# Eighteen up pairs in seven block products instead of fourteen, with one low part made by ScalarE and an accumulating DMA

## The chip, the core and the metric

The kernel runs on one core of a Trainium2 chip. Its engines are TensorE (PE in the rows), VectorE (DVE), ScalarE (ACT), GpSimd (POOL) and SyncE (SP); the last two here mostly issue DMAs. The metric is the device time of one execution in microseconds (us), lower is better. Three runs of the kernel before took 881.33, 883.00 and 883.19 us.

## The reference, cut to what matters

One layer of a streaming encoder over 512 tokens of width 1024, all in float32. The change lies in its last part, the feed-forward block:

```python
h = rmsnorm(x, ffn_pre_norm[l])
up = causal_dwconv(h @ w_ffn_up[l], ffn_conv_w[l], ffn_conv_b[l])   # 1024 -> 2 * 3072
f_gate, f_val = jnp.split(up, 2, axis=-1)
f = (jax.nn.gelu(f_gate, approximate=True) * f_val) @ w_ffn_down[l]
x = x + rmsnorm(f, ffn_post_norm[l])
```

## The kernel before, in words

Every float32 product is made of three products in a faster 32-bit format (float32r): an operand x is split into a high part (x rounded) and a low part (x minus the high part), and high x high, high x low and low x high are summed in PSUM. ScalarE makes the high part with a copy that rounds, VectorE the low part with a subtraction. Activations are kept split; weights come from HBM and are split on the way (`split`, `low` at L951).

The 6144 columns of the up projection are worked off in 24 pairs of 128 gate columns and 128 value columns. The weights of a pair are four blocks of 128 x 512: a11 and a12 (gate, first and second half of the 1024 inputs), a21 and a22 (value). The pairs 0 and 1 run ahead of the stretch looked at here. Each pair from 2 on is done in one of two ways:

- in eight block products (`eight`, L1049): each of the two outputs takes 24 matmuls of 512 columns, 48 in all, in four slots; a11 with a12, and a21 with a22, are split as one 1024-wide block;
- in seven block products (`seven`, L1014), a Winograd scheme on the 2 x 2 blocks of weights and activations: the sums s1, s2, s3, s4 of weight blocks stand beside a11, a12 and a22, the sums of activations are made once (`comb`), and each of the seven products is 12 matmuls of 256 columns, 84 in all. Six of them run in the pair's six slots in the order a11, s2, s4, s3, a12, s1; the seventh, with a22 (`last_product`, L998, the matmuls named ps<-L,a), runs within the next pair, and goes into a PSUM half that VectorE has read before (L1046).

`seven_of` (L908) says which pairs are done in seven: pair n = 4 + i unless i % 3 = 2, so 14 pairs; 2, 3, 6, 9, 12, 15, 18 and 21 are done in eight. A loop over the pairs (L1111) runs the slots; in each it splits the block that is used five slots later (`w_split`, L954; the split parts lie in a ring of six). For a seven, `w_split` also adds s2 = s1 + a11 on VectorE (L965, at a11), s4 = s2 + a12 (L968, at s2), and at s3 splits a22 as well, on ScalarE and VectorE. In slot 0 of pair n the weights of pair n + 2 are loaded (`pair_load`, L922, 1 MB, on SyncE's queue, L926) into the tile H that held those of pair n, so the load waits until all that was in it has been read. `pair_sums` (L931) makes s1 and s3 of pair n + 2 by DMA: a load from HBM on SyncE's queue (L940) and a second one that adds to it on GpSimd's (L942).

The outputs of a pair are finished while the next one runs: `gate_part` (a depthwise conv, ScalarE one tap, VectorE two, L226), `gelu_part`, `last_product`, `value_part` (L1002: one add, L1005, for a seven, the conv, and the product of gate and value, L866). For a seven VectorE also puts the partial products together with 256-wide adds (L1031, L1044, L1045, L1046). After pair 23 the down projection follows; `down_turn` finishes that pair in it.

TensorE and here ScalarE run in program order. VectorE, SyncE and GpSimd run in an order that a planner sets when the program is built: an instruction is put where the planner expects its inputs, ahead of ones that come earlier in the program if these are expected later. On the chip each engine's queue is then strictly in order. Waits between engines and for the reuse of buffers are set by the framework.

Of the kernel before, what the change touches and what calls it, by code (L numbers as in the profile page):

```python
# [8 lines left out]
F32 = mybir.dt.float32  # L9
# [3 lines left out]
ALU = mybir.AluOpType  # L13
# [9 lines left out]
NF = FF // P  # L23
# [33 lines left out]
def block_kernel(ctx: ExitStack, tc, x, slabs, wgate, pc, rows, out):  # L57
    nc = tc.nc
    V, A, PE = (InOrder(tc, e) for e in (nc.vector, nc.scalar, nc.tensor))
    G = nc.gpsimd  # L60
# [9 lines left out]
    def ps():  # L70
        return psum.tile([P, S], F32, tag="ps", name="ps")
# [16 lines left out]
    def mm3(acc, lhi, llo, rhi, rlo, start, stop):  # L88
        mm(acc, lhi, rhi, start, False)
        mm(acc, lhi, rlo, False, False)  # L90
        mm(acc, llo, rhi, False, stop)
# [770 lines left out]
    def f_gate(gt):  # L862
        A.activation(gt, gt, AF.Gelu_apprx_tanh)
# [34 lines left out]
    def block_product(out, w, b, start=False):  # L898

        for k in range(HK):  # L900
            c = slice(k * P, (k + 1) * P)
            for e, (u, v) in enumerate(((0, 0), (0, 1), (1, 0))):
                PE.matmul(out, lhsT=w[u][:, c], rhs=b[v][:, k, :], start=start and k == e == 0,
                          stop=k == HK - 1 and e == 2, skip_group_check=not start)

    seven_of = [False] * 4 + [i % 3 != 2 for i in range(NF - 4)] + [False]  # L908
    ORDER = "a11", "s2", "s4", "s3", "a12", "s1"
    blocks = [(n, q) for n in range(PLAIN, NF + 1)  # L910
              for q in (ORDER if seven_of[n] else ("a11", "a12", "a21", "a22"))]
# [32 lines left out]
    def place(kind, i):  # L944

        key = kind, i // 2
        if key not in room:
            room[key] = wts.tile([P, D], F32 if kind == "raw" else F32R, tag=kind, name=kind)
        return room[key][:, i % 2 * S:(i % 2 + 1) * S]

    def low(lo, src, hi):  # L951
        V.tensor_sub(lo, src, hi.bitcast(F32))  # L952

    def w_split(g):  # L954

        if g >= len(blocks):
            return
        n, q = blocks[g]
        b, i = blk[n], g % RING
        both = [place(kind, i) for kind in ("whi", "wlo")]  # L960
        b["w" + q] = both
        if seven_of[n]:
            if q == "a11":
                b["s2"] = place("raw", 4)
                V.tensor_add(b["s2"], b["s1"], b["a11"])  # L965
            elif q == "s2":
                b["s4"] = place("raw", 5)
                V.tensor_add(b["s4"], b["s2"], b["a12"])  # L968
            A.copy(both[0], b[q])
            low(both[1], b[q], both[0])  # L970
            if q == "s3":
                if not spare:
                    spare.append(work.tile([P, 2, 2, S], F32R, tag="M", name="a22", bufs=1))
                b["wa22"] = [spare[0][:, n % 2, e, :] for e in range(2)]
                A.copy(b["wa22"][0], b["a22"])
                low(b["wa22"][1], b["a22"], b["wa22"][0])
        elif q in ("a12", "a22"):
            hi, lo = (room[kind, i // 2] for kind in ("whi", "wlo"))
            src = b["raw"][:, 0:D] if q == "a12" else b["raw"][:, D:2 * D]
            A.copy(hi, src)  # L980
            low(lo, src, hi)
            if n == NF:
                splits[DOWN_SLAB + (q == "a22")] = hi, lo
# [7 lines left out]
    def gate_part(n):  # L991
        p = pr[n]
        p["g"] = conv(p["oa"], pcs[:, C_FCW + 3 * n:C_FCW + 3 * n + 3], C_FCB + n, 3)

    def gelu_part(n):
        f_gate(pr[n]["g"])

    def last_product(n):  # L998
        if seven_of[n]:
            block_product(pr[n]["z"][:, T1], blk[n]["wa22"], comb[3])  # L1000

    def value_part(n):  # L1002
        p = pr.pop(n)
        if seven_of[n]:
            V.tensor_add(p["ob"][:, T0], p["u2"], p["z"][:, T1])  # L1005
            w = negw[:, 3 * n:3 * n + 3]
        else:
            w = pcs[:, C_FCW + 3 * (NF + n):C_FCW + 3 * (NF + n) + 3]
        vt = conv(p["ob"], w, C_FCB + NF + n, 3)
        f_done(n, p["g"], vt)  # L1010
# [38 lines left out]
    def eight(n, old):  # L1049
        p = pr.setdefault(n, {})  # L1050
        for e, o in enumerate(("oa", "ob")):
            p[o] = acc = ps()
            for h in range(2):
                w = blk[n]["wa%d%d" % (e + 1, h + 1)]
                for k in range(HK):
                    c = slice(k * P, (k + 1) * P)
                    mm3(acc, w[0][:, c], w[1][:, c], h2T[0][:, HK * h + k, :],
                        h2T[1][:, HK * h + k, :], h == k == 0, h == 1 and k == HK - 1)
                if old:
                    if e == h == 0:  # L1060
                        gate_part(old)
                    elif e == 0:
                        gelu_part(old)
                        last_product(old)
                    elif h == 0:
                        value_part(old)
                yield

# [19 lines left out]
    for i in range(PLAIN):  # L1088
        acc = up_product()
        if i == 0:  # L1090
            pair_load(PLAIN)
            pair_load(PLAIN + 1)
        gt = conv(acc, pcs[:, C_FCW + 3 * i:C_FCW + 3 * i + 3], C_FCB + i, 3)
        if i == 0:
            w_split(0)
            w_split(1)
            for m in range(4):
                h_sum(m)
        else:
            for g in range(2, RING - 1):  # L1100
                w_split(g)
            h_split(1)
            h_split(2)
        acc = up_product()
        vt = conv(acc, pcs[:, C_FCW + 3 * (NF + i):C_FCW + 3 * (NF + i) + 3], C_FCB + NF + i, 3)
        f_gate(gt)
        f_done(i, gt, vt)
# [3 lines left out]
    for n in range(PLAIN, NF):  # L1111
        for slot, _ in enumerate((seven if seven_of[n] else eight)(n, old)):
            w_split(g + RING - 1)
            g += 1
            if slot == 0:
                pair_load(n + 2)
                pair_sums(n + 2)
            if n == PLAIN and slot in (1, 2):
                h_split(3 * (slot - 1))
            if n < NF - 1:  # L1120
                continue
            if slot == 2:
                stream.update(load=DOWN_SLAB + 2, split=DOWN_SLAB + 2, use=DOWN_SLAB)
                end[0] = slabs.shape[0]
                load_slab()
            elif slot == 3:
                f_split(0)
                f_split(1)
            elif slot == 5:
                f_split(2)  # L1130
                f_split(3)
        old = n
# [100 lines left out]
```

## Time and profile before

| | |
|---|---|
| median of three runs | 883.0 us |
| the profiled execution, its own time | 882.06 us |
| its span, first to last instruction | 880.4 us |
| TensorE busy | 864.7 us (98%) |
| VectorE busy | 587.4 us (67%) |
| ScalarE busy | 433.6 us (49%) |
| GpSimd busy | 28.4 us (3%) |
| granted TensorE clock, mean share of full speed | 0.996 |
| share of the chain that ended last: TensorE, VectorE, DMA, ScalarE | 75%, 11%, 7%, 5% |

A busy share is an average over stages with different limits, and matmuls are pipelined with modelled ends, so a busy TensorE is not one at its peak. The chain of work is followed back from the last instruction, at each step to what released it. Outside the stretch of pairs 4 to 23 the change touches nothing but the hand-over to the down projection.

### The profile page before, as it was taken

The page shows a single profiled execution, that of the slowest core. Times are in us where ns is not written, and L with a number is a line of the kernel's source. Part 1 is how long each engine was busy: PE and PEld are TensorE (multiplying, and loading weights), DVE is VectorE, ACT ScalarE, POOL GpSimd, SP SyncE. Part 2 cuts the span into 40 slices and gives each one's busy share as a digit, 9 for nine tenths or more (in the row PEclk, how much of TensorE's full clock was granted, in tenths as well). Part 3 has the DMA queues.
Part 4 walks back from the last instruction along what each step waited for, and adds up shares of the span by engine and source line. Part 5 has one row for each costly group of instructions (what it writes and reads, how often), then busy time and mean ns, then how long its engine had stood idle before and what let it go on. Part 6 is the DMA issues. An engine that isn't in the chain of part 4 may idle for free.

```text
span 880.4 us, 11591 instructions
## 1 busy us (share of the span) xinstructions
PE 864.7 (98%) x4554; PEld 739.7 (84%) x4554; DVE 587.4 (67%) x909; ACT 433.6 (49%) x714; POOL 28.4 (3%) x44
## 2 busy tenths in 40 slices
PE   7999999999999999999999999999999999999996
PEld 6888887888878888888888989889999899888885
DVE  6777657987875553444466797878978898743225
ACT  6444545578574443322365565445545556633222
POOL 0000000000000000000000101011011000000000
PEclk9999999999999999999999999999999999999999
DMA  6242223222334422222251837466556543422212
GB/s 225 96 146 96 96 94 110 90 84 79 119 103 174 154 96 96 87 99 101 97 191 25 212 127 195 126 180 170 165 144 181 156 127 113 144 96 95 96 48 96
DMA packets 36007, 108.47 MB, mean 123 GB/s; under 512 B 3632, under 2 KB 6896, under 8 KB 35440
## 3 DMA queue, kind: packets, MB, share of 16 engines
q1 hardware_dynamic: 30864, 99.34, 32.7%
q0 software_dynamic: 5088, 8.39, 5.7%
q8 instruction: 35, 0.57, 0.2%
q14 instruction: 20, 0.16, 0.1%
HBM read 103.49 MB, written 2.13 MB: 120 GB/s over the span
## 4 chain that ended last, share of the span: by engine, by line
PE 75%; DVE 11%; DMA 7%; ACT 5%; issue 2%; SPq 0%; DVEq 0%; ACTq 0%
PE ps L53 75%; DMA H<-slabs 5%; DVE wlo L952 2%; DVE tmp L226 2%; ACT whi L53 1%; DVE wlo L183 1%; ACT L L53 1%; DVE L L644 1%; DMA raw<-slabs 1%; ACT tmp L53 1%; DVE tmp L662 1%; DVE raw L965 0%; DMA wg<-wgate 0%; DVE L L638 0%; ACT junk L247 0%
## 5 line engine op out<-in xcount | busy, mean ns | idle before, releaser
L53 PE MATMUL ps<-H,whi 128*128 128x512 f32 x720 | 224.8, 395 | 0.4 <-DVE H L53 0.4
L183 DVE TENSOR_TENSOR wlo<-raw,whi 128x1024 fp32r<-128x1024 f32 x93 | 113.6, 1223 | 117.3 <-ACT whi L53 115.0
L53 ACT CAST whi<-raw 128x1024 fp32r<-128x1024 f32 (+1 forms) x144 | 127.5, 891 | 100.2 <-PE ps L53 96.6
L53 PE MATMUL ps<-C,whi 128*128 128x256 f32 (+1 forms) x656 | 166.5, 335 | 0.1
L53 PEld LDWEIGHTS ps<-H,whi 128*128 128x128 f32 x720 | 134.3, 188 | 30.3 <-issue 2.4
L53 PE MATMUL ps<-H,wlo 128*128 128x512 f32 x352 | 137.5, 391 | 0.4 <-DVE wlo L183 0.4
L53 PEld LDWEIGHTS ps<-C,whi 128*128 128x128 f32 x656 | 112.0, 190 | 12.6 <-DVE quad L1031 0.3
L53 PE MATMUL ps<-C,wlo 128*128 128x512 f32 (+1 forms) x360 | 122.2, 339 | 0.0
L53 PE MATMUL ps<-L,whi 128*128 128x256 f32 (+1 forms) x400 | 87.2, 300 | 0.0
L53 PE MATMUL ps<-whi,H 128*128 128x512 f32 x256 | 81.5, 394 | 0.0
L226 DVE SCALAR_TENSOR_TENSOR tmp<-ps,pcs,tmp 128x511 f32<-128x511 f32 (+2 forms) x100 | 74.5, 745 | 8.1 <-ACT tmp L53 7.2
L53 PEld LDWEIGHTS ps<-H,wlo 128*128 128x128 f32 x352 | 66.2, 188 | 15.3 <-DVE wlo L183 1.2
L53 PEld LDWEIGHTS ps<-C,wlo 128*128 128x128 f32 x360 | 68.3, 190 | 7.6
L53 PEld LDWEIGHTS ps<-L,whi 128*128 128x128 f32 x400 | 64.4, 191 | 2.5
L53 PEld LDWEIGHTS ps<-whi,H 128*128 128x128 f32 x256 | 48.1, 188 | 10.4 <-issue 0.5
L53 ACT ACTIVATE tmp<-tmp 128x512 f32<-128x512 f32 x36 | 22.7, 632 | 55.3 <-DVE tmp L226 55.3
L53 PE MATMUL ps<-wlo,H 128*128 128x512 f32 x128 | 49.8, 389 | 0.0
L952 DVE TENSOR_TENSOR wlo<-H,whi 128x512 fp32r<-128x512 f32 (+1 forms) x46 | 41.1, 894 | 9.7 <-ACT whi L53 9.6
L53 PE MATMUL ps<-L,wlo 128*128 128x256 f32 x168 | 47.5, 283 | 0.0
L53 ACT ACTIVATE tmp<-ps,halfb 128x512 f32<-128x512 f32 x32 | 21.5, 687 | 49.6 <-PE ps L53 49.6
L53 ACT ACTIVATE tmp<-ps,pcs 128x512 f32<-128x512 f32 x40 | 31.0, 776 | 27.9 <-PE ps L53 27.9
L53 PE MATMUL ps<-Y,whi 128*128 128x512 f32 x128 | 40.5, 397 | 0.2 <-DVE Y L200 0.2
(207 smaller groups left out, 1315.3 us busy)
## 6 DMA issues: line engine op xcount, KB each, us to landing
raw<-slabs SPq DMA_DIRECT2D x103, 512.0 KB, 3.2
H<-slabs SPq DMA_DIRECT2D x23, 1024.0 KB, 5.4
raw<-slabs SPq DMA_DIRECT2D x23, 256.0 KB, 3.8
raw<-slabs POOLq DMA_DIRECT2D x23, 256.0 KB, 6.5
quad<-x SPq DMA_DIRECT2D x8, 512.0 KB, 4.2
M<-acsD SPq DMA_DIRECT2D x4, 1024.0 KB, 4.6
out<-tmp SPq DMA_DIRECT2D x8, 256.0 KB, 2.0
third<-slabs SPq DMA_DIRECT2D x5, 256.0 KB, 6.3
```

What stands on the lines that cost most here:

```text
L53: return lambda *args, **kw: self.tc.keep_in_program_order(op(*args, **kw))
L183: V.tensor_sub(*late.pop(0))
L226: V.scalar_tensor_tensor(out=t[:, d:], in0=acc[:, :S - d], scalar=w[:, taps - 1 - d:taps - d], in1=t[:, d:], op0=ALU.mult, op1=ALU.add)
L644: V.tensor_tensor_scan(out=qq[:, e, :], data0=aa[:, e, :], data1=uu[:, e, :], initial=0.0, op0=ALU.mult, op1=ALU.add)
L662: V.tensor_mul(gl, gl, hs[i // 4][:, i % 4, :])
L952: V.tensor_sub(lo, src, hi.bitcast(F32))
```

## The change

`seven_of` is changed so that of the pairs 4 to 23 only 10 and 17 are done in eight products: 18 pairs in seven instead of 14, in three runs of six. In every seven the low part of a22 is no longer VectorE's subtraction: ScalarE writes minus the high part into the place of the low part, and a DMA issued by GpSimd adds a22 to it, from on-chip memory to on-chip memory. In a pair done in eight products the `last_product` of the pair before comes one slot later, after the third of four, and with it `value_part`, after the fourth.

```diff
-    seven_of = [False] * 4 + [i % 3 != 2 for i in range(NF - 4)] + [False]
+    seven_of = [False] * 4 + [i not in (6, 13) for i in range(NF - 4)] + [False]
...
                 b["wa22"] = [spare[0][:, n % 2, e, :] for e in range(2)]
-                A.copy(b["wa22"][0], b["a22"])
-                low(b["wa22"][1], b["a22"], b["wa22"][0])
+
+                hi, lo = b["wa22"]
+                A.copy(hi, b["a22"])
+                A.mul(lo, hi.bitcast(F32), -1.0)
+                G.dma_start(out=lo.bitcast(F32), in_=b["a22"], accum_op=ALU.add)
...
                     elif e == 0:
                         gelu_part(old)
+                    elif h == 0:
                         last_product(old)
-                    elif h == 0:
+                    else:
                         value_part(old)
```

## Rows read from the trace of the kernel before

**Rows 1.** Timeline of TensorE: start us, duration us, engine, line, operation, tiles, shape, count.

```profile
531.84 0.40 PE L53 MATMUL ps<-C,whi 128*128 128x256 f32 x2
...
584.47 0.61 PE L53 MATMUL ps<-C,whi 128*128 128x512 f32 x2
...
585.15 0.61 PE L53 MATMUL ps<-C,whi 128*128 128x512 f32 x2
...
589.60 1.69 PE L53 MATMUL ps<-L,a 128*128 128x256 f32 x12 [0.89 <-DVE tmp L1046]
...
596.59 0.40 PE L53 MATMUL ps<-C,whi 128*128 128x256 f32 x2
...
596.95 0.40 PE L53 MATMUL ps<-C,whi 128*128 128x256 f32 x2
...
741.21 0.28 PE L53 MATMUL ps<-L,wlo 128*128 128x256 f32 x1
```

**Rows 2.** Windows from eight to eight: span, busy us per engine, clock, DMA share.

```profile
583.08:615.49 32.41, 31.52 (x219) 29.14 (x218) 27.15 (x46) 16.78 (x30) 3.40 (x4) 1.00 0.57 162
615.49:646.57 31.08, 31.08 (x219) 29.16 (x218) 26.48 (x45) 18.01 (x31) 3.42 (x4) 1.00 0.68 180
...
sum 159.70, PE 156.83 PEld 145.64 DVE 134.67 ACT 82.63 POOL 17.06; mean PE 31.37 PEld 29.13 DVE 26.93 ACT 16.53 POOL 3.41
```

**Rows 3.** Timeline of VectorE, 570 to 590 us; in brackets its wait before.

```profile
570.91 1.29 DVE L952 TENSOR_TENSOR wlo<-raw,whi 128x512 fp32r<-128x512 f32 x2 [0.34 <-ACT whi L53]
...
573.38 0.74 DVE L226 SCALAR_TENSOR_TENSOR tmp<-ps,pcs,tmp 128x510 f32<-128x510 f32 x1
574.04 0.68 DVE L952 TENSOR_TENSOR a<-H,a 128x512 fp32r<-128x512 f32 x1
574.64 0.68 DVE L866 TENSOR_TENSOR H<-tmp 128x512 f32<-128x512 f32 x1
575.24 0.41 DVE L1044 TENSOR_TENSOR quad<-quad,ps 128x256 f32<-128x256 f32 x1
575.57 0.69 DVE L952 TENSOR_TENSOR wlo<-H,whi 128x512 fp32r<-128x512 f32 x1
...
577.53 0.75 DVE L226 SCALAR_TENSOR_TENSOR tmp<-tmp,pcs 128x511 f32<-128x511 f32 x1 [0.61 <-ACT tmp L53]
...
581.25 1.23 DVE L952 TENSOR_TENSOR wlo<-H,whi 128x1024 fp32r<-128x1024 f32 x1 [1.37 <-ACT whi L53]
582.39 0.41 DVE L1005 TENSOR_TENSOR tmp<-quad,ps 128x256 f32<-128x256 f32 x1
584.07 0.69 DVE L965 TENSOR_TENSOR raw<-raw,H 128x512 f32<-128x512 f32 x1 [1.26 <-DMA H<-slabs]
...
589.46 0.68 DVE L952 TENSOR_TENSOR wlo<-H,whi 128x512 fp32r<-128x512 f32 x1
```

**Rows 4.** Waits, 530 to 710 us: who for whom, total, times, longest.

```profile
DVE raw L965 <- DMA H<-slabs: 14.8, 9, 2.7
```

**Rows 5.** Timeline of ScalarE, SyncE and GpSimd between 572 and 577 us.

```profile
572.48 0.62 ACT L53 CAST a<-H 128x512 fp32r<-128x512 f32 x1
573.00 0.37 ACT L53 COPY tmp<-ps 128x256 f32<-128x256 f32 x1
...
576.28 0.38 SPq L926 DMA_DIRECT2D H<-slabs  x1
...
575.78 0.84 POOL L942 DMA_DIRECT2D raw<-slabs  x1 [6.03 <-DMA raw<-slabs]
```

**Rows 6.** Single DMAs issued at 540.39, 567.75, 638.54 and 638.17: KB, us to landing.

```profile
third<-slabs POOLq DMA_DIRECT2D x1, 256.0 KB, 4.0
...
H<-slabs SPq DMA_DIRECT2D x1, 1024.0 KB, 5.2
...
H<-slabs SPq DMA_DIRECT2D x1, 1024.0 KB, 7.9
third<-slabs POOLq DMA_DIRECT2D x1, 256.0 KB, 8.1
```

## The prediction

> **What bounds the kernel now.** I read the busy table first, then the stretch of the change by thirds, then single engines in it. The table of busy time says TensorE 98%, VectorE 67%, but matmuls are pipelined, so 98% doesn't say that TensorE never waits. The stretch that matters is the block products of the up pairs 4 to 23. The first matmul of pair 4 starts at 531.84 and the last of pair 23 starts at 741.21 and takes 0.12 us: 209.5 us [rows 1]. There three 512-column matmuls take 0.68 us (0.2267 each) and three of 256 columns 0.36 us (0.12 each) [rows 1]. A pair in eight products is 48 x 0.2267 = 10.88 us, one in seven is 84 x 0.12 = 10.08 us. Before, 14 sevens and 6 eights, less one block of twelve matmuls (1.44 us) that pair 23 leaves to the down stage, need 141.1 + 65.3 - 1.4 = 205.0 us. So 4.5 us of the 209.5 are stalls.
>
> Where they come from is seen by comparing groups of three pairs (two sevens and an eight; TensorE needs 31.04 us for them). The five whole groups sum to 159.70 us, 155.2 needed; one took 32.41, the next 31.08 [rows 2]. In the slow one TensorE stands 0.89 us before the twelve matmuls of `last_product`, released by VectorE's L1046 [rows 1]. VectorE was late because it is as full as TensorE: its queue is in order, and in the same group it waited 1.26 us at L965 for the pair load (tile H) to land, and 1.37 us for ScalarE's cast of an eight [rows 3]. Over 530 to 710 us the pair load cost it 14.8 us in nine waits [rows 4], 2.6 us a group.
>
> VectorE's budget, from start to start in its timeline [rows 3]: a low part 0.60, a conv tap 0.66, a 256-wide add 0.33, an add of the block sums 0.69, the product L866 0.60, a 1024-wide low part 1.14. A seven: 7 lows 4.20 + 4 taps 2.64 + L866 0.60 + L965 and L968 1.38 + five 256-wide adds 1.65 = 10.47, and it stands 0.34 and 0.61 us for ScalarE in each: 11.42 us. An eight: 2.28 + 2.64 + 0.60 + 1.37 of waiting = 6.89. Two sevens and an eight: 29.7, with 2.6 of load waits 32.3. That is the 32.41. A seven costs VectorE more than TensorE (11.42 against 10.08); the eights pay it back. For all twenty pairs this budget gives 14 x 11.42 + 6 x 6.89 + 6 x 2.6 = 216.8, and the stretch took 209.5: VectorE enters with splits done ahead and leaves with a lag, worth 7.3 us. I keep this 7.3 for the kernel after.
>
> **The change part by part.** Four eights become sevens: TensorE's need falls by 4 x 0.80 = 3.2 us, to 18 x 10.08 + 2 x 10.88 - 1.4 = 201.8 us.
>
> In all 18 sevens the low part of the last block leaves VectorE: 11.42 - 0.60 = 10.82 us. ScalarE gets a multiply of the size of its cast, which with the next start behind it takes 573.00 - 572.48 = 0.52 us [rows 5]. It is busy 82.63 of 159.70 us in the five groups [rows 2] and idles for VectorE soon after, so nothing is charged; without that cover it would be 18 x 0.52 = 9.4 us. Behind it in ScalarE's queue stand the copy of the output half and the cast of a12, whose low part starts on VectorE at 575.57, 2.6 us later [rows 3]. The multiply waits for the `last_product` two pairs back, as the cast of the same block just before it does already.
>
> VectorE after: 18 x 10.82 + 2 x 6.89 = 208.5, less 7.3 = 201.2, plus load waits. The waits of today come with the eights; two are left, so 0 to 5.2 us, and I take the middle, 2.6: 203.8 us. TensorE's 201.8 is below it, so VectorE stays the bound by 2 us. In the eights `last_product` comes one block (2.72 us) later; the 0.89 us stall is covered by that, and what is late next is VectorE's total. I give it no gain of its own.
>
> Sum against the profiled execution: 209.5 - 203.8 = 5.7 us less; 882.06 - 5.7 = 876.4. That execution lies 0.9 us under the median of the three runs and inside their spread (881.33 to 883.19), so I say 876.5. This case's own range is 874.4 (TensorE's floor, 201.8) to 879.0 (all 5.2 us of waits).
>
> The new DMA is the edit with two answers. It isn't in the trace; the nearest rows are the accumulating loads of the same 256 KB, 4.0 to 8.1 us from issue to landing [rows 6]. It can only start when the multiply is done, about 573.00 + 0.52 = 573.5 in the pair shown, so it lands at 577.5 to 581.6. GpSimd's queue is moved past too: it stood 6.03 us until 575.78 for a load behind which this DMA may queue [rows 5]. The load of the pair after next overwrites the tile that the DMA reads, so SyncE must wait for it. Today that load issues at 576.28, when the a12 low part is done [rows 5]; with one low part less it would be 575.7. So it is 1.8 to 5.9 us later than it would be, and the loads of the sums in SyncE's queue behind it as well. Who waits is L965, which adds a11 to s1, and every VectorE instruction behind it. I take no charge, because in a run of sevens a11's low part of the pair after next is a whole seven and two blocks behind the a12 low part: 10.82 x 8/6 = 14.4 us, against at most 5.9 + 7.9 = 13.8 of delay and load [rows 6]. This holds only if the planner issues L965 near that low part. The other end is the first rival.
>
> On the accumulate a rule weighs the other way from the rows. The Trainium skill (DMA: Bandwidth & Descriptors, "Anatomy of one DMA — SWDGE (gpsimd) path") gives a GpSimd-issued DMA about 2.0 us plus its bytes at 436 GB/s, an estimate of 2.6 us for 256 KB; by it the pair load would be 0.4 us late, not 1.8 to 5.9, and the forecast would stand. The rows (4.0 at least) disagree. Against the change speaks the same page, "Issuing engines are not separate DMA queues": whoever issues, the same 16 DMA engines carry it; the trace agrees: a pair load issued with no accumulate under way landed after 5.2 us, one issued just behind an accumulate after 7.9 [rows 6].
>
> **The rivals.** First, slower: the pair load becomes VectorE's wait in every seven. For it speaks that the planner reorders VectorE: L965 at 584.07 runs 5.4 us before the low part of its a11 (589.46), right behind L1005, and waits there today [rows 3]. Left in that place, VectorE would reach it at 584.07 - 1.26 - 0.60 = 582.2. The load would land at 573.5 + 4.0 + 6.6 (the middle of 5.2 and 7.9) = 584.1: 1.9 us of waiting; between the ends 0.5 to 7.3. Twelve pairs stand in the inside of the three runs (6 to 9, 13 to 16, 20 to 23): 12 x 1.9 = 22.8 us, 203.8 + 22.8 = 226.6, so 882.06 + 17.1 = 899. It decides from 0.5 us a pair (12 x 0.5 = 5.7, all of the gain). Against it: these hoisted places all lie in or just before eights, where VectorE had room; a run of six sevens has none.
>
> Second, no change: VectorE keeps what it is given. If a seven stands for ScalarE 0.3 us longer than today, since the multiply delays the cast of a12 and GpSimd's place in the queue delays s1, 18 x 0.3 = 5.4 us are gone: 882. For it speaks that VectorE stands for ScalarE in every seven already; against it that ScalarE is half idle.
>
> Third, TensorE alone bounds: the L965 fills the 0.61 us in which VectorE stands for ScalarE, no load wait is left, and the time is at the floor or a little under, 874.
>
> **How the numbers follow.** Forecast (with the third) 0.55, of which 0.05 below 874; first rival 0.33; second 0.12. Within 0.2% (1.8 us, about what a measurement of this kernel can tell from no change) is the second. Faster 0.55, same 0.12, slower 0.33. The range goes from 874 to 899: 0.05 lies below and some 0.15, the first rival's upper half, above.
>
> **What would show it.** Right: the starts of pairs 4 and the end of 23 some 204 us apart, sevens 10.1 to 10.3 us long inside a run, no stall before `last_product` in an eight, and L965's waits for H no more than 5 us in all. The first rival: L965 waits of 1 us and more in pairs 6 to 9, the H loads issued when GpSimd's DMA lands instead of behind the a12 low part, TensorE standing in the second half of each run. The second: 209 us again with the same H waits and longer waits of VectorE for ScalarE. The forecast is wrong if L965 stands two blocks or more before its low part in the runs of sevens.

## The result, and the profile after

The kernel after took 921.19 us in the median of six runs (918.6 to 924.01), the kernel before 882.16 us in six runs beside them (878.19 to 883.82). The ratio is 1.045, 95% interval 1.042 to 1.0487: slower, and 45 us from the forecast of 876.5, outside its range of 874 to 899.

The profiled execution of after took 924.01 us, its span is 922.3 us. From the page: busy time, share of the span and count of each engine, and the shares of the chain that ended last.

```profile
PE 873.5 (95%) x4698; PEld 752.5 (82%) x4698; DVE 595.4 (65%) x939; ACT 455.1 (49%) x760; POOL 51.0 (6%) x70
...
PE 58%; DVE 15%; DMA 15%; ACT 6%; issue 4%; SPq 0%; POOL 0%; DVEq 0%; POOLq 0%; ACTq 0%
```

TensorE falls from 98% to 95% and VectorE from 67% to 65%; ScalarE stays at 49%, GpSimd goes from 3% to 6%. The chain tells it: DMA has 15% where it had 7%, VectorE 15% where it had 11%, TensorE 58% where it had 75%. Time went into waiting for transfers.

The stretch of the up pairs 4 to 23 as one window of after, in the columns of [rows 2]: span, then busy us of TensorE, weight loads, VectorE, ScalarE and GpSimd, the granted clock, the DMA share and GB/s.

```profile
533.70:782.80 249.10, 214.72 (x1597) 206.28 (x1596) 187.48 (x330) 131.65 (x238) 41.29 (x48) 0.97 0.66 171
```

The stretch took 249.1 us, before 209.5 [rows 1]: 39.6 of the 42.0 us between the two profiled executions. VectorE is busy 187.5 of it and idle 61.6. Who waits for whom in it (total us, times, longest), the answer to [rows 4]:

```profile
POOL raw L942 <- DMA raw<-slabs: 126.3, 21, 10.3
...
DVE raw L965 <- DMA H<-slabs: 51.5, 14, 7.2
PE ps L53 <- DVE quad L1034: 24.5, 12, 3.1
```

The wait of L965 for the pair load was 14.8 us in nine times [rows 4] and is 51.5 us in fourteen: 36.7 us more, about all of the 39.6. Behind it stands TensorE, which waits for L1034 (L1031 before; the lines from `last_product` on moved by three). One turn of this can be followed through the timelines of ScalarE, GpSimd, SyncE and VectorE; start us, duration us, in brackets the wait before:

```profile
568.79 0.63 ACT L53 ACTIVATE a<-a 128x512 fp32r<-128x512 f32 x1
...
570.35 0.85 POOL L942 DMA_DIRECT2D raw<-slabs  x1 [5.18 <-DMA raw<-slabs]
570.94 1.14 POOL L979 DMA_DIRECT2D a<-H  x1
...
576.54 0.38 SPq L926 DMA_DIRECT2D H<-slabs  x1
...
582.46 0.69 DVE L965 TENSOR_TENSOR raw<-raw,H 128x512 f32<-128x512 f32 x1 [3.38 <-DMA H<-slabs]
...
589.21 0.69 DVE L952 TENSOR_TENSOR wlo<-H,whi 128x512 fp32r<-128x512 f32 x1
```

ScalarE's multiply ends at 569.4. GpSimd stands 5.18 us for a load of a sum that comes ahead in its queue, and issues the accumulating DMA at 570.94. From the view of single DMAs (KB, us from issue to landing) that DMA took 5.5 us and the pair load issued at 576.54 took 5.8:

```profile
a<-H POOLq DMA_DIRECT2D x1, 256.0 KB, 5.5
...
H<-slabs SPq DMA_DIRECT2D x1, 1024.0 KB, 5.8
```

So the DMA lands at 576.44, the load of the tile that it read is issued 0.1 us later and lands at 582.34, and L965, the next in VectorE's queue, has stood 3.38 us by then. What needs the data in time, the low part of the same a11, comes only at 589.21, 6.8 us after the add. Of the 18 pair loads issued in the stretch, 16 are issued within 0.1 us of the landing of that DMA. That is 0.5 to 6.3 us, on average 3.1, behind the end of the a12 low part, where each load of a seven was issued in the kernel before [rows 3, 5].

The 1.14 us that GpSimd shows for the DMA are not its transfer. The Trainium skill (Perfetto Trace Analysis, "Summary: the profiler window per engine type") says that such a slice ends when the descriptors are made, with the movement of data outside it; the rows agree: 1.14 us of slice, 5.5 us from issue to landing.

### The profile page after: what moved, and what is told of

Its sections match the earlier page's. It is cut to its first block, busy times and chain, and to the rows that moved or that the text cites. A ratio compares the mean times of both kernels' runs of the same rounds, so it can differ in the third digit from the quotient of the medians.

```text
span 922.3 us, 12091 instructions
## 1 busy us (share of the span) xinstructions
PE 873.5 (95%) x4698; PEld 752.5 (82%) x4698; DVE 595.4 (65%) x939; ACT 455.1 (49%) x760; POOL 51.0 (6%) x70
## 4 chain that ended last, share of the span: by engine, by line
PE 58%; DVE 15%; DMA 15%; ACT 6%; issue 4%; SPq 0%; POOL 0%; DVEq 0%; POOLq 0%; ACTq 0%
PE ps L53 58%; DMA H<-slabs 8%; DVE tmp L226 4%; DVE wlo L952 3%; DMA raw<-slabs 3%; DMA a<-H 2%; DMA Y<-C 2%; ACT tmp L53 1%; ACT L L53 1%; DMA third<-slabs 1%; ACT whi L53 1%; DVE wlo L183 1%; DVE L L644 1%; ACT L53 1%; DVE raw L965 1%
## 5 line engine op out<-in xcount | busy, mean ns | idle before, releaser
L53 PE MATMUL ps<-H,whi 128*128 128x512 f32 x720 | 226.6, 398 | 2.0 <-DVE H L53 2.0
L53 ACT CAST whi<-raw 128x1024 fp32r<-128x1024 f32 (+1 forms) x159 | 136.2, 864 | 103.8 <-PE ps L53 96.7
L53 PE MATMUL ps<-C,whi 128*128 128x256 f32 (+1 forms) x624 | 148.7, 323 | 24.5 <-DVE quad L1034 24.5
L53 PE MATMUL ps<-C,wlo 128*128 128x256 f32 (+1 forms) x344 | 113.1, 329 | 3.9 <-DVE wlo L952 3.9
L53 PE MATMUL ps<-L,whi 128*128 128x256 f32 (+1 forms) x496 | 108.6, 304 | 0.0
L53 PEld LDWEIGHTS ps<-L,whi 128*128 128x128 f32 x496 | 82.9, 200 | 2.5
L226 DVE SCALAR_TENSOR_TENSOR tmp<-ps,pcs,tmp 128x511 f32<-128x511 f32 (+2 forms) x84 | 62.4, 744 | 10.5 <-ACT tmp L53 9.7
L53 PE MATMUL ps<-L,wlo 128*128 128x256 f32 x216 | 62.8, 291 | 1.4 <-DVE wlo L952 1.4
L942 POOL DMA_DIRECT2D raw<-slabs x30 | 27.9, 950 | 611.3 <-DMA raw<-slabs 587.6
L53 ACT ACTIVATE tmp<-tmp,pcs 128x512 f32<-128x512 f32 x18 | 14.7, 817 | 64.4 <-DVE tmp L1048 60.8
L952 DVE TENSOR_TENSOR wlo<-raw,whi 128x512 fp32r<-128x512 f32 x66 | 44.3, 684 | 3.1 <-ACT whi L53 3.1
```

The source lines that it names most:

```text
L53: return lambda *args, **kw: self.tc.keep_in_program_order(op(*args, **kw))
L226: V.scalar_tensor_tensor(out=t[:, d:], in0=acc[:, :S - d], scalar=w[:, taps - 1 - d:taps - d], in1=t[:, d:], op0=ALU.mult, op1=ALU.add)
L942: G.dma_start(out=b[q], in_=drawn(n, *two), accum_op=ALU.add)
```

## The experiments

My theory after the result: L965 stands some 7 us ahead of its low part, and the late pair load makes it VectorE's wait; either cutting the load loose from the DMA or moving the add back takes most of the loss away, and both together give the forecast. (The first half of this was not borne out, as the runs below show.) The rivals: the four more sevens are too much for VectorE by themselves; the DMA waits in GpSimd's queue, and its place there is the cause; the DMAs' traffic slows the pair load; the later slot of `last_product` does it.

The table has all kernels, for the sections below. "Budget" is that of the prediction for VectorE (11.42 us a seven, 10.82 with the low part off VectorE, 6.89 an eight without load waits, less 7.3), but not below TensorE's need, plus the L965 waits that the run's own trace shows. "Stretch" is measured, from the first matmul of pair 4 to the last of pair 23 of the profiled execution.

| kernel | sevens, a22 low part | also changed | L965 waits for H | budget + waits | stretch | median us | ratio, 95% interval |
|---|---|---|---|---|---|---|---|
| before | 14, VectorE | | 14.8 | 208.7 to 219.8 | 209.5 | 882.16 | 1 |
| after | 18, DMA | late `last_product` (as all below) | 51.5 | 252.7 | 249.1 | 921.19 | 1.042 to 1.0487 |
| e12_late_last | 14, VectorE | | 25.8 | 219.7 to 230.8 | 218.6 | 890.8 | 1.0057 to 1.0148 |
| e1_dve_low | 18, VectorE | | 7.2 | 219.2 | 213.1 | 891.2 | 1.0085 to 1.0208 |
| e2_dma_14 | 14, DMA | | 33.0 | 218.5 to 238.0 | 231.6 | 904.62 | 1.0255 to 1.0326 |
| e3_own_copy | 18, DMA | copy | 28.1 | 229.3 | 227.8 | 896.77 | 1.0177 to 1.0216 |
| e4_pin_add | 18, DMA | adds held | 21.2 | 222.4 | 226.6 | 894.32 | 1.0138 to 1.0195 |
| e5_own_pin | 18, DMA | copy, adds held | 0 | 201.8 | 202.8 | 874.28 | 0.9915 to 0.9951 |
| e6_dve_pin | 18, VectorE | adds held | 0 | 212.0 | 213.8 | 886.01 | 1.0045 to 1.0099 |
| e7_14_dve_pin | 14, VectorE | adds held | 0 | 205.0 | 205.2 | 877.09 | 0.9952 to 0.9979 |
| e8_no_adds | 18, DMA | sums' second loads left out | 7.7 | 208.9 | 206.3 | 880.1 | 0.9971 to 1.0006 |
| e9_pool_pin | 18, DMA | GpSimd's order held | 42.3 | 243.5 | 241.3 | 913.22 | 1.0323 to 1.0414 |
| e10_pool_add_pin | 18, DMA | GpSimd's order and adds held | 5.2 | 206.4 | 204.8 | 876.55 | 0.9917 to 0.9964 |
| e11_all | 18, DMA | copy, GpSimd's order and adds held | 0 | 201.8 | 202.8 | 874.2 | 0.9902 to 0.995 |

Where waits add to a kernel that TensorE would otherwise bound (14 sevens), two sums are given: the waits on VectorE's own budget (193.9, or 185.5 with the DMA), and on TensorE's 205.0. For 18 sevens VectorE's budget is used; TensorE's 201.8 stands where it is the larger. The kernels from e1 to e4, from e5 to e8 and from e9 to e12 ran together on one chip each; the kernel before took 879.86, 880.89 and 881.56 us beside them and 882.16 beside after, so a difference between two of these groups is good to some 2 us, and the ratios are each against the kernel before of its own group.

### Cutting the load loose, and moving the add back

The DMA reads a copy of a22 that ScalarE makes in a place that is free until pair 22, so that the pair load doesn't wait for it:

```diff
-                G.dma_start(out=lo.bitcast(F32), in_=b["a22"], accum_op=ALU.add)
+                own = b["a22"]
+                if n < 22:
+                    own = fY[1][:, 6 + n % 2, :]
+                    A.copy(own, b["a22"])
+                G.dma_start(out=lo.bitcast(F32), in_=own, accum_op=ALU.add)
```

> The changed kernel, but for pairs 4 to 21 ScalarE first copies a22 into a free place (18 copies of 0.52 us more on ScalarE) and the accumulating DMA reads that, so the pair load has not to wait for the DMA. DMA count and bytes are unchanged. Theory A: H loads issue behind the a12 low part again, L965 waits for H fall from 51.5 to under 20 us, and the time falls to 878 to 892 us. Rival C (the DMA's traffic and GpSimd's full queue slow everything): H loads land as late as now, and the time stays above 910 us.

The adds are kept in program order on VectorE, that is just ahead of their own low parts:

```diff
-                V.tensor_add(b["s2"], b["s1"], b["a11"])
+                tc.keep_in_program_order(V.tensor_add(b["s2"], b["s1"], b["a11"]))
...
-                V.tensor_add(b["s4"], b["s2"], b["a12"])
+                tc.keep_in_program_order(V.tensor_add(b["s4"], b["s2"], b["a12"]))
```

> The changed kernel with the adds L965 and L968 pinned in VectorE's queue behind what precedes them in the program, so that the planner can't put them two blocks ahead of the low part that needs them. Theory A with the place of the add as its condition: the load is as late as now (H issues at the landing of the DMA), but VectorE does other work meanwhile; L965 waits fall below 20 us and the time to 880 to 895 us. If the load itself is too late whatever the place: L965 or the a11 cast still wait 30 us or more and the time stays above 905 us.

Both edits together:

> Both cures together: the DMA reads a copy of a22 (as in e3_own_copy, 896.8 us), and the adds L965 and L968 are pinned behind what precedes them in the program (as in e4_pin_add, 894.3 us). If the late load and the early place of the add are one chain, either cure takes most of the same waits away, and what is left is something else: 885 to 894 us with L965 waits for H under 10 us. If the two cures act on different waits, the gains add up (24 + 27 us from 921) to 870 to 880 us. If GpSimd's queue and the traffic are the rest (rival C), it stays at 890 us or more with few waits for H.

The copy gave 896.77 us and the held adds 894.32, some 24 and 27 us under after; together they gave 874.28 (873.75 to 877.47, nine runs), 0.9933 of the kernel before beside it (880.89) and 47 us under after. The waits of the copy, of the held adds, and the stretch of both together with two rows of its VectorE timeline:

```profile
DVE raw L965 <- DMA H<-slabs: 28.1, 13, 5.3
```

```profile
ACT whi L53 <- DMA H<-slabs: 35.4, 10, 8.1
DVE raw L965 <- DMA H<-slabs: 21.2, 7, 5.3
```

```profile
530.82:733.57 202.75, 202.39 (x1597) 198.19 (x1596) 185.00 (x328) 142.83 (x255) 41.36 (x48) 1.00 0.83 210
...
574.71 0.69 DVE L965 TENSOR_TENSOR raw<-raw,H 128x512 f32<-128x512 f32 x1
575.32 0.69 DVE L952 TENSOR_TENSOR wlo<-H,whi 128x512 fp32r<-128x512 f32 x1
```

With the copy alone the add stands where it was, and waits 28.1 us for a load that is no longer held up by the DMA; the expectation of waits under 20 us and at most 892 us was missed. With the add alone moved back, the load is late even for the low part: ScalarE's cast of a11 waits 35.4 us for it, the sign of a load that is too late whatever the place, though the time came within the 880 to 895 expected of the other theory. With both, L965 stands 0.6 us ahead of its low part, no wait of L965 for H is left, and TensorE is busy 202.39 of 202.75 us. Neither edit took most of the loss: the gains of 24 and 27 us nearly add up to the 47, the second of the three outcomes expected for both together.

Why the load is so late with the adds held is seen in one turn of e4_pin_add, from the timelines of ScalarE, GpSimd and SyncE:

```profile
570.26 0.63 ACT L53 ACTIVATE a<-a 128x512 fp32r<-128x512 f32 x1
...
578.11 0.84 POOL L942 DMA_DIRECT2D third<-slabs  x1 [9.19 <-DMA third<-slabs]
578.71 1.13 POOL L979 DMA_DIRECT2D a<-H  x1
...
572.00 0.38 SPq L926 DMA_DIRECT2D H<-slabs  x1
572.49 0.41 SPq L940 DMA_DIRECT2D third<-slabs  x1
...
584.16 0.38 SPq L926 DMA_DIRECT2D H<-slabs  x1
```

The multiply ends at 570.9, but its DMA is issued at 578.71, behind a load of a sum (tile third) that GpSimd awaits for 9.19 us. That sum's first load stood on SyncE's queue right behind the pair load of 572.00, which itself had waited for the landing of the a22 DMA before. So one late pair load makes the next one later: within each of the three runs of sevens the delay of the load behind the a12 low part grows, from 3.5 to 11.7 us, from 1.5 to 11.8 and from 3.0 to 11.2. The DMA stands 4.3 us in GpSimd's queue on average, 2.4 in after.

### GpSimd's queue and the traffic

GpSimd's loads of the sums are held in program order, behind the a22 DMA that comes ahead of them:

```diff
-            G.dma_start(out=b[q], in_=drawn(n, *two), accum_op=ALU.add)
+            tc.keep_in_program_order(G.dma_start(out=b[q], in_=drawn(n, *two), accum_op=ALU.add))
```

> The changed kernel, complete, with the accumulating DMAs of pair_sums pinned in GpSimd's queue behind the a22 accumulate that precedes them in the program; DMA count, bytes and VectorE's order are free as before. Theory A with the queue as its largest part: the a22 DMA no longer stands behind an add that waits for its first load, issues within 0.5 us of the multiply, and the time falls most of the way that leaving the adds out gave (880): 882 to 897 us. If leaving the adds out helped by the traffic it saved, the order alone gives little: 908 us or more.

The same with the adds held:

> GpSimd's adds pinned as in e9_pool_pin, and VectorE's adds L965 and L968 pinned as in e4_pin_add; no copy of a22. If queue, flight of the DMA and early place of the add are all of the loss: 872 to 880 us, as e5_own_pin (874.3), since the load then leaves some 5 us after the multiply and its user stands a block later. If the wait of the load for the DMA's flight (5 us) still shows: 882 to 892 us.

The sums' second loads left out, so that s1 and s3 hold only one of their two blocks; nothing is then ahead of the a22 DMA in GpSimd's queue, and 256 KB less is moved for each sum:

```diff
-        for q, one, two in adds:
-            G.dma_start(out=b[q], in_=drawn(n, *two), accum_op=ALU.add)
```

> The changed kernel without the accumulating DMAs of pair_sums (s1 and s3 hold one addend only, so 36 DMAs of 256 KB and their waits on GpSimd's queue are left out). GpSimd's queue then holds only the a22 accumulates. Theory A with the queue as a part of it: the a22 DMA issues at once instead of 2.9 us after the multiply (mean), H issues that much earlier, the L965 waits fall from 51.5 to 25 us or less and the time from 921 to 880 to 895 us. If the queue doesn't matter, the H loads stay as late after the multiply as now (about 8.5 us) and the time above 910 us.

All three edits (copy, adds and GpSimd's order):

> e5_own_pin (copy of a22 for the DMA, L965 and L968 pinned, 874.3 us) with GpSimd's adds pinned as well. In e5_own_pin the loads no longer wait for the a22 DMA, so the queue of GpSimd delays only the seventh product's operand, which has time: the same within 3 us (872 to 877 us). If the queue still costs there, 868 to 871 us; if the later adds make s1 late, 880 us or more.

Holding GpSimd's order did to the DMA what it should: it was issued 0.4 us after the multiply's end on average, not 2.4, and landed 3.6 us later in the median, not 5.4. Yet the time was 913.22 us, 8 under after: the expectation of 882 to 897 was missed, and its other outcome came, 908 us or more. Its waits, and its DMA issues (count, KB each, median us to landing):

```profile
DVE raw L965 <- DMA H<-slabs: 42.3, 14, 7.7
...
H<-slabs SPq DMA_DIRECT2D x19, 1024.0 KB, 7.3
...
a<-H POOLq DMA_DIRECT2D x18, 256.0 KB, 3.6
```

The pair load, issued earlier, now took 7.3 us, against 5.7 in after. Without the sums' second loads it took 4.9 with the a22 DMA just as quick, and the time was 880.1:

```profile
H<-slabs SPq DMA_DIRECT2D x19, 1024.0 KB, 4.9
...
a<-H POOLq DMA_DIRECT2D x18, 256.0 KB, 3.6
```

So with the add in its early place the queue's delay is not the cause by itself: what is won there is largely paid back while the sums' loads run beside the pair load. In e9_pool_pin the five pair loads during which no accumulate of a sum was under way took 4.7 to 4.8 us, the other fourteen 5.1 to 11.8. In both kernels the add stands 5.4 us or more ahead of its low part in the run, as in after. With GpSimd's order and the adds held, the time was 876.55 us, 18 under e4_pin_add with the adds alone. Its pair loads are issued 1.4 to 4.3 us behind the a12 low part, and the delay doesn't grow within a run: in e4_pin_add the queue is most of what was left of the loss. With the copy too it was 874.2, the same as without GpSimd's order (874.28). Once the add stands late and the queue is short, pair loads of 8.1 us do little harm.

```profile
ACT whi L53 <- DMA H<-slabs: 13.3, 6, 5.9
...
DVE raw L965 <- DMA H<-slabs: 5.2, 2, 2.7
...
H<-slabs SPq DMA_DIRECT2D x19, 1024.0 KB, 8.1
```

What remains of L965's waits there, two of them, lies at the two eights.

### One part of the change alone

Eighteen sevens with the low part on VectorE:

```diff
-                A.mul(lo, hi.bitcast(F32), -1.0)
-                G.dma_start(out=lo.bitcast(F32), in_=b["a22"], accum_op=ALU.add)
+                low(lo, b["a22"], hi)
```

> The changed kernel with the low part of a22 back on VectorE (18 pairs in seven, last_product in the eights one slot later, no accumulating DMA for a22). Theory A (the pair load waits for the accumulating DMA, and VectorE waits for the load at L965): the load leaves again when the a12 low part is done, L965 waits for H fall from 51.5 us to under 20 us, and the time is what VectorE's budget gives, 18 x 11.42 + 2 x 6.89 + 2.6 - 7.3 = 214.7 us for pairs 4 to 23, so about 887 us (880 to 895). Rival B (six sevens in a run are too much for VectorE and ScalarE whatever makes the low part): 910 us or more, with few waits for H.

Fourteen sevens with the DMA:

```diff
-    seven_of = [False] * 4 + [i not in (6, 13) for i in range(NF - 4)] + [False]
+    seven_of = [False] * 4 + [i % 3 != 2 for i in range(NF - 4)] + [False]
```

> The changed kernel with the old choice of pairs (14 in seven, an eight after every two), a22's low part still by ScalarE and the accumulating DMA. Theory A: every seven's load is still late by the DMA, so L965 waits for H rise from before's 14.8 us to 25 us or more and the time is 890 to 910 us, slower than before. Rival B (it is the number of sevens in a run): VectorE has 14 x 0.60 = 8.4 us less to do and the time is 876 to 883 us.

Both of these edits, so that of the change only the later `last_product` is left:

> The kernel before with last_product in the eights one slot later, and nothing else. TensorE stands some 3.4 us in all before last_product in the eights; the later slot covers them. If these stalls are TensorE's own: 876 to 879 us beside 880 of before. If VectorE's total is what is late next, as the prediction had it: no change, 879 to 882 us.

Eighteen and fourteen sevens with the low part on VectorE and the adds held:

> 18 pairs in seven, a22's low part on VectorE, the adds L965 and L968 pinned. It is e1_dve_low (885.7 to 896.2 us) without its 7.2 us of waits for H. Theory A (VectorE's budget): 18 x 11.42 + 2 x 6.89 - 7.3 = 212.0 us for the pairs, so about 882 to 886 us. If the adds had filled gaps in which VectorE waits for ScalarE, pinning costs instead: 888 us or more.

> The kernel before (14 in seven, low part on VectorE) with the adds L965 and L968 pinned and last_product in the eights one slot later. Theory A: before's 14.8 us of waits for H and its 3.4 us of stalls before last_product go, TensorE's need of 205.0 us for the pairs bounds: 876 to 879 us beside some 880 of before. If those waits are only moved to the cast of a11 on ScalarE or to the adds behind: 880 us or more.

The first two came as expected of the theory (891.2 and 904.62 us), so the sevens in a run are not the cause by themselves. The later `last_product` alone costs 9 us (890.8 against 881.56), which neither expectation had: L965 waits 25.8 us in eleven of its adds, 14.8 in nine before.

```profile
DVE raw L965 <- DMA H<-slabs: 25.8, 11, 3.0
```

From the four medians without held adds, the DMA adds 14 us at fourteen sevens (904.62 against 890.8) and 30 at eighteen (921.19 against 891.2); the four more sevens add nothing measurable with VectorE's low part (891.2 against 890.8, of which more below) and 17 with the DMA. With the adds held the late `last_product` shows no such cost: fourteen sevens take 877.09 us, 3.8 under the kernel before (880.89). No run holds the adds with `last_product` in its old slot. With the adds held, the four more sevens cost 9 us on VectorE (886.01), and the DMA with the copy wins 12 (874.28). So what the change was meant to bring, the fewer matmuls of four more sevens, is 2.8 us (877.09 to 874.28), beside the 3.2 that the prediction gave for TensorE; the other 3.8 of the 6.6 won over the kernel before are there at fourteen sevens with the adds held. The stretches of eighteen and of fourteen sevens on VectorE, adds held:

```profile
532.55:746.38 213.83, 204.36 (x1598) 198.67 (x1596) 193.92 (x342) 122.98 (x222) 26.37 (x31) 1.00 0.65 177
```

```profile
531.32:736.51 205.19, 205.19 (x1454) 193.70 (x1452) 176.42 (x296) 114.61 (x195) 19.57 (x23) 1.00 0.58 164
```

In the one VectorE bounds: 213.83 us by 212.0 of budget. In the other TensorE never stands: 205.19 of 205.19 us, the need of fourteen sevens worked out in the prediction as 205.0.

Two things stay open here. The four runs of eighteen sevens on VectorE lie in two groups, 885.65 and 886.21, 896.19 and 896.21; the profiled execution is the first (213.1 us of stretch, 7.2 us of waits), what the others wait for isn't known, and the median between the groups isn't used for more than its rough place. And in the run with only the later `last_product` VectorE's add stands as far ahead of its low part as before (5.4 and 8.5 us against 5.4 and 8.2), but every third pair load takes 8.4 to 9.5 us where it took 5.1 to 9.2; why the later slot lengthens it was not tried.

## Why the prediction was wrong, point by point

**What bounds, and VectorE's budget: right.** The budget was fitted to the kernel before alone, and with the L965 waits of each trace added it gives the stretch of after and of nine other kernels of eighteen sevens within 6.1 us, eight of these ten within 3.6; the two off by more are e1_dve_low (6.1 too long) and e4_pin_add (4.2 too short, with ScalarE's 35.4 us of waits not in it). Without any waits it holds best: 212.0 worked out, 213.8 measured; TensorE's 201.8 and 205.0 against 202.8 and 205.2. Fed with what it left out, 51.5 us of waits, the prediction's 201.2 gives 252.7 for after, measured 249.1.

**The step that failed: "I take no charge" for the new DMA.** It was taken on the ground that the low part of the next a11 is 14.4 us behind, with the condition that the planner issues L965 near that low part. It doesn't, and what was put at nothing came to 51.5 us of waits where the forecast held 2.6. In after the adds of the runs stand 5.4 to 8.5 us ahead of that low part, and [rows 3] had shown the distance: 5.4 us at 584.07, and in the kernel before it is 5.4 or 8.2 us in nearly every seven. This is the sign of being wrong that the prediction named: two blocks or more. The argument against it, that these places lie in or just before eights, was what let the condition pass; in e7_14_dve_pin the six eights are there, the adds are held, and L965 has no wait for H. Of the 14.4 us some 6 to 9 were left, against 1.8 to 5.9 of delay and 5.2 to 7.9 of load in the prediction's own terms, 7.0 to 13.8 together. The step has a second fault, in that 5.9 of delay was taken as the most: in after the delay was 0.5 to 6.3 us, but where the condition is true and nothing else is changed (e4_pin_add) it was 1.5 to 11.8, on average 7.4, ScalarE's cast of a11 waits 35.4 us and the time is 894.32. What the sum left out is the wait in GpSimd's queue, 4.3 us there on average. Why the planner puts the add there was not tried, only what it costs.

**The first rival: its mechanism is what happened, its price was too low.** L965 waits of more than 1 us in pair after pair, pair loads issued at the landing of GpSimd's DMA, TensorE standing behind: the marks are in the rows above, though TensorE stands all through the runs and not only in their second half. It was priced at 1.9 us in twelve pairs, 22.8 us; measured are 51.5 us in fourteen, 3.7 each. The terms: from the multiply's end to the landing it took 4.0 us, measured are 2.4 in GpSimd's queue and 5.4 of flight, 7.8; for the load it took 6.6, measured is 5.7. The 6.03 us wait of GpSimd [rows 5] was named and not charged. With both terms the rival's 1.9 would have been 1.9 + 3.8 - 0.9 = 4.8, an upper estimate, since VectorE reaches the add later too. At the 51.5 measured, less the 2.6 that the forecast held, 203.8 + 48.9 = 252.7 and a time of 925, beside 924.01 in the profiled execution.

**The low end of the accumulate.** The estimate of 2.6 us from the Trainium skill's page (DMA: Bandwidth & Descriptors) was set against 4.0 at least from the rows. The on-chip accumulate took 3.6 us in the median in e8_no_adds and e9_pool_pin, where no sum's accumulate is ahead of it, and 5.4 in after: the rows of the loads were nearer.

**The multiply on ScalarE at nothing: holds.** In e5_own_pin and e11_all ScalarE has it, and the copy besides, and the stretch is within 1 us of TensorE's need. So does the 10.8 us of VectorE's low parts: e6_dve_pin to e5_own_pin is 11.7 us.

**"No gain of its own" for the later `last_product`: wrong.** It lost 9 us alone, with more waits of the same add; with the adds held no loss is seen.

**The forecast itself.** With the add late the kernel takes 894.32 us; with the load's delay cut as well, by GpSimd's order, the copy or both, 876.55, 874.28 and 874.2, beside 876.5. The nearness is partly luck: the forecast kept 2.6 us of load waits and VectorE as the bound, while the last two have no wait of L965 and TensorE bounds them, and holding the adds helps the kernel before too (877.09). The third case, TensorE alone, is the nearest of all to the last two: 874.

## What to carry to other kernels

When a transfer becomes later, look up in the trace where the first instruction that reads it stands in its engine's queue, not where its result is needed: the slack is counted from the first, and an early place that costs 1 or 2 us today is the price of every microsecond of delay tomorrow. Before a DMA is put in the place of an engine's instruction, follow what it reads: the buffer is now held until the DMA lands, with the queue ahead of it and its flight. And where an order made by a planner is in doubt, holding the one instruction in place is the cheapest experiment; here it was worth 27 us alone and, with a copy that frees the buffer, turned 39 us lost into 6.6 won. And try such an order on the kernel before as well: 3.8 of the 6.6 us were to be had there without the four more sevens and the DMA.

## What the runs showed of the hardware

TensorE's clock fell behind some of the waits. After a stand of 2.93 us in after (no matmul busy from 625.6 to 628.5) the granted clock was at half in the windows from 629 on, while TensorE was busy throughout, and at full again in that of 633. In the windows of 1 us the granted clock is the third figure from the end; 0.50 is the lower level, 1.2 of 2.4 GHz:

```profile
627.00:628.00 1.00, 0.00 (x0) 0.00 (x0) 1.00 (x2) 0.38 (x1) 0.01 (x1) 1.00 0.71 283
...
629.00:630.00 1.00, 1.00 (x8) 1.00 (x7) 1.00 (x3) 1.00 (x3) 0.00 (x0) 0.52 0.94 317
630.00:631.00 1.00, 1.00 (x6) 1.00 (x6) 1.00 (x3) 0.99 (x2) 0.00 (x0) 0.50 0.96 162
631.00:632.00 1.00, 1.00 (x7) 1.00 (x6) 1.00 (x2) 0.98 (x3) 0.00 (x0) 0.50 1.03 285
...
633.00:634.00 1.00, 1.00 (x11) 1.00 (x10) 1.00 (x3) 0.00 (x0) 0.56 (x1) 1.00 0.44 154
```

In a busy microsecond at half clock 6 or 7 matmuls of 256 columns were under way at some time, at full clock 11. In the stretch TensorE stands thirteen times for 1.7 us or more, and after five of them the clock was at half for a while; the length of the stand does not decide it alone, since it fell after one of 1.88 us (from 753.3) and not after one of 2.12 (from 611.0). Over the stretch of after the clock is 0.97, where before it is 1.00, which is some 8 us of TensorE's time at the most, an estimate from the 0.97 of 249.1 us; TensorE shows 214.7 us busy for a need of 201.8. How much of the time this cost was not measured apart: where VectorE is the later one, a slower TensorE can be hidden. The Trainium skill (TensorE: Matmul & The Clock Gate, "HAM oscillation — how this bites in real kernels") tells of a matmul kernel that waits for its next operand again and again and starts at the low clock after each wait; here it was so after five of the thirteen.

The same 1 MB pair load took 4.9 us in the median without the sums' second loads, 5.7 in after, 7.8 in e5_own_pin and 7.3, 8.1 and 7.6 in e9 to e11, where more of those loads ran beside it.
